# Keeping the residual transposed: a hybrid decoder layer rewritten to feature-major order

## The chip, the cores and the metric

The kernel runs on the 8 cores of one Trainium2 chip. Each core handles one prompt of 2048 tokens and 16 of the 128 sample sequences, with all the weights. The metric is the device time of the slowest core in microseconds (us), as the median over runs. A program on all 8 cores has a second, slower state in some runs, in which cores of one die show a lower granted clock than the others. Those runs are marked slow and are not compared here.

Engine names in the profile: PE is the matrix engine and PEld its weight loads, DVE the vector engine, ACT the scalar (activation) engine, POOL the GpSimd engine, and SP the engine that here only issues transfers. `L376` is line 376 of that kernel. "PEclk" is the clock granted to PE, as a fraction of full speed.

## The reference

One decoder layer: a norm, an input projection (1024 to 2048), two mixers side by side (pooling means, and a gated short convolution), an output projection, a second norm, a squared-ReLU MLP (1024 to 4096 to 1024), and a final norm. Cut to what matters:

```python
def rmsnorm(x, g):
    return x * rsqrt(mean(x * x, axis=-1) + EPS) * g

hn = rmsnorm(x, norm1_g)
u, bg, cg, hc = split(einsum('btd,de->bte', hn, w_in), 4)       # each 512 wide
ya = pool_mixer(u)          # means over the last 2, 4, 8, 16 rows minus u, times pool_w
yb = bg * conv3(cg * hc)    # 3 taps along the tokens
x = x + concat([ya, yb]) @ w_out
hn = rmsnorm(x, norm2_g)
x = x + square(relu(hn @ w1)) @ w2
y = rmsnorm(x, final_g)
```

Per core this is 16 meta + 2048 prompt + 64 sample tokens.

## The kernel before

The residual lies token-major: 128 tokens on the partitions, 1024 features along each row, 17 tiles, of which the last (the 64 sample tokens) is half filled. A norm is then a row sum, which ACT makes together with the square. But the kernel's projections take the features on the partitions, so each normalized tile goes through 8 transposes on PE.

```python
def stats(src, pn, src_keys, junk, junk_key):          # one norm: a row sum on ACT
    P.add("scalar", lambda e: e.activation(out=junk[0:pn, :], in_=src, func=AF.Square,
                                           accum_out=ss[0:pn, slot:slot + 1]), ...)
    ...                                                # Sqrt on ACT, reciprocal on DVE

def transpose_to_fm(hn, hn_key, pn, gT, dst, dst_keys):
    for k in range(8):
        P.add("tensor", lambda e, k=k: e.transpose(out=psT[tb][:, k * 128:k * 128 + pn],
                                                   in_=hn[:, k * 128:(k + 1) * 128], ...), ...)
    ...                                                # DVE: times the gain, out of PSUM

# the pooling sums and their last two steps run on POOL
P.add("gpsimd", lambda e, ...: e.tensor_tensor(out=dstb[:, a0:L], in0=cur_src[:, a0:L],
                                               in1=cur_src[:, a0 - step:L - step], op=ALU.add), ...)

def load_block(b):                                     # MLP weights, block b of 4
    P.dma("gpsimd", ... W1B[i] ...)
    P.dma("gpsimd", ... W2B[i] ...)

load_block(0)
w1_step(0, pending)
pop_pending(pending, 8)
load_block(1)                                          # only after the first step's work is queued
```

All weights come through the casting queue that POOL issues to. The cuts are marked by `...`.

## Time and profile before

| | before |
|---|---|
| time, median of 6 runs | 728.21 us (727.29 to 729.3) |
| profiled span, slowest core | 725.3 us |
| PE busy | 675.0 us, 93% |
| MLP's first matmul | 246.9 us |
| MLP, first to last matmul | 470.5 us |
| after the last matmul | 7.9 us |

The page of the kernel before. The rows of digits are 40 equal slices of the span, each digit the busy share in tenths.

```profile
span 725.3 us, 10524 instructions; the slowest of 8 cores (720.2 to 725.3 us)
...
PE 675.0 (93%) x3705; PEld 320.7 (44%) x3705; DVE 321.8 (44%) x440; ACT 239.3 (33%) x456; POOL 99.4 (14%) x121
...
PE   0699899899899999999999999999999999999995
...
POOL 4184055055073000000000000000000000000000
PEclk9999999999999999999999999999999999999998
...
PE 89%; DMA 4%; ACT 2%; issue 2%; DVE 2%; SPq 0%; ACTq 0%; DVEq 0%
```

PE is the bound: it is busy in 93% of the span, its row is 9 nearly everywhere after the first two slices, and the chain of waits (the last line) goes 89% through it. PEclk is 9 up to the last slice, so little is lost to the clock either. POOL is busy almost only in the first 13 slices, which are the mixer.

Two consecutive pieces of the chain of waits (start, length, what), from the mixer:

```profile
102.00 6.91 PE psall L363 x32
108.91 0.45 PE psall L353 x8
```

Here 32 matmuls of 512 columns take 6.91 us, which is 216 ns each, and 8 transposes of 128 columns take 0.45 us, which is 56 ns each. In stretches without waits, the starts of neighbouring matmuls stand 29 ns apart at 64 columns and 216 at 512 in this kernel's trace (216 for the half-filled tile too). All of these fit columns / 2.4 + 2.5 ns within 0.5 ns, and estimates below are made with that. Each matmul has a weight load of its own, 98 ns long in the mean of its records, and the short ones still start 29 and 56 ns apart.

Busy time by stage (window, its length, then busy us of each engine, granted clock, share of the DMA engines, GB/s):

```profile
0.00:246.90 246.90, 207.77 (x1305) 104.29 (x1305) 115.83 (x173) 129.86 (x240) 93.98 (x115) 0.99 0.37 76
246.90:717.40 470.50, 467.20 (x2400) 216.45 (x2400) 201.96 (x263) 108.11 (x213) 5.39 (x7) 1.00 0.25 48
717.40:725.30 7.90, 0.00 (x0) 0.00 (x0) 3.98 (x5) 1.35 (x3) 0.00 (x0) 0.69 0.49 200
```

In the MLP, PE is idle for only 3.3 of 470.5 us. In the mixer it is idle for 39 of 246.9 us, most of it while the first loads and norms run.

The timeline around a POOL addition (start, length, engine, line, operation):

```profile
111.90 4.25 POOL L474 TENSOR_TENSOR big<-big 128x526 f32<-128x526 f32 x3
...
112.41 1.36 DVE L515 SCALAR_TENSOR_TENSOR big<-big 128x512 f32<-128x512 f32 x1
...
113.70 1.54 DVE L512 SCALAR_TENSOR_TENSOR big<-big 128x512 f32<-128x512 f32 x1
```

POOL adds here from 111.90 to 116.15, three times in a row, 1.42 us each. The two DVE operations beside them, which read two operands from SBUF, take 1.36 and 1.54 us. Elsewhere, with POOL quiet, the same DVE operation took 0.75 us (at 127.2 us), and a POOL addition with DVE quiet took 1.04 us (at 98.2 us). Beside each other, one addition and one DVE operation so get done about every 1.45 us, which is less than the 1.79 us of one after the other.

### The profile page before, as it was taken

The numbers are of one execution on the slowest core, as the hardware profiler recorded it, in microseconds if no ns is written. First come the engines' busy times: TensorE is split into PE (matmuls) and PEld (weight loads), VectorE is DVE, ScalarE is ACT, GpSimd is POOL, SyncE is SP. The second block draws the span as 40 slices with busy tenths as digits, with TensorE's granted clock in tenths as the row PEclk, the third lists the DMA queues.
The fourth block names the chain that finished last, engine by engine and source line by source line (L and its number), as shares of the span: only waits on it lengthen the run. The fifth ranks groups of instructions, "written<-read, shape, count | busy, mean of one in ns | idle before, by whom it ended". The sixth has DMA issues, their size and how long they took to land.

```text
span 725.3 us, 10524 instructions; the slowest of 8 cores (720.2 to 725.3 us)
## 1 busy us (share of the span) xinstructions
PE 675.0 (93%) x3705; PEld 320.7 (44%) x3705; DVE 321.8 (44%) x440; ACT 239.3 (33%) x456; POOL 99.4 (14%) x121
## 2 busy tenths in 40 slices
PE   0699899899899999999999999999999999999995
PEld 0355444444444454444444444444444444444442
DVE  0326527628536453333343333333433333364566
ACT  3655556556443531202012021102220202333432
POOL 4184055055073000000000000000000000000000
PEclk9999999999999999999999999999999999999998
DMA  8994400300002899001643000607000000020224
GB/s 198 190 188 67 148 1 1 117 0 2 1 1 30 122 156 160 30 0 19 98 62 56 0 1 1 107 10 117 1 1 0 2 1 1 1 95 37 88 89 171
DMA packets 19682, 42.98 MB, mean 59 GB/s; under 512 B 1503, under 2 KB 5631, under 8 KB 19616
## 3 DMA queue, kind: packets, MB, share of 16 engines
q0 software_dynamic: 14176, 23.22, 21.2%
q1 hardware_dynamic: 5456, 19.11, 7.7%
q8 instruction: 30, 0.49, 0.3%
q14 instruction: 20, 0.16, 0.1%
HBM read 56.64 MB, written 9.24 MB: 91 GB/s over the span
## 4 chain that ended last, share of the span: by engine, by line
PE 89%; DMA 4%; ACT 2%; issue 2%; DVE 2%; SPq 0%; ACTq 0%; DVEq 0%
PE psall L363 48%; PE psall L743 32%; PE psall L634 6%; DMA big<-w 2%; PE psall L353 2%; DMA big<-xp 2%; DVE big L357 1%; ACT big L346 1%; ACT big L334 1%; ACT big L621 0%; DVE big L762 0%; ACT big L726 0%; ACT big L752 0%; PE psall L595 0%; PE psall L589 0%
## 5 line engine op out<-in xcount | busy, mean ns | idle before, releaser
L363 PE MATMUL psall<-big 128*128 128x512 bf16 (+2 forms) x2036 | 361.5, 335 | 10.9 <-ACT big L726 3.0
L363 PEld LDWEIGHTS psall<-big 128*128 128x128 bf16 x2036 | 167.1, 98 | 194.9 <-issue 18.2
L743 PE MATMUL psall<-big 128*128 128x512 bf16 (+1 forms) x1088 | 238.0, 379 | 0.0
L726 ACT ACTIVATE big<-psall 128x512 f32<-128x512 f32 (+1 forms) x160 | 83.3, 522 | 319.4 <-PE psall L363 310.1
L743 PEld LDWEIGHTS psall<-big 128*128 128x128 bf16 (+1 forms) x1088 | 106.6, 98 | 127.6 <-issue 1.7
L728 DVE TENSOR_TENSOR big<-big 128x512 bf16<-128x512 f32 (+1 forms) x160 | 95.2, 599 | 136.1 <-ACT big L726 135.3
L748 DVE TENSOR_TENSOR big<-psall,big 128x1024 f32<-128x1024 f32 (+1 forms) x68 | 83.3, 1224 | 129.3 <-PE psall L743 127.1
L634 PE MATMUL psall<-big 128*128 128x512 bf16 (+1 forms) x272 | 61.1, 385 | 3.7 <-DVE big L357 3.6
L474 POOL TENSOR_TENSOR big<-big 128x512 f32<-128x512 f32 (+13 forms) x50 | 50.5, 1009 | 79.7 <-ACT big L498 68.5
L357 DVE TENSOR_TENSOR big<-psall,big 128x1024 bf16<-128x1024 bf16 (+2 forms) x35 | 39.8, 1163 | 26.9 <-PE psall L353 26.8
L334 ACT ACTIVATE big<-big 128x1024 bf16<-128x1024 f32 (+2 forms) x35 | 36.9, 1056 | 44.0 <-DVE big L639 35.8
L346 ACT ACTIVATE big<-big 128x1024 bf16<-128x1024 f32 (+2 forms) x35 | 39.4, 1145 | 14.3 <-PE psall L353 9.4
L634 PEld LDWEIGHTS psall<-big 128*128 128x128 bf16 (+1 forms) x272 | 26.9, 100 | 37.3 <-issue 7.4
L353 PE MATMUL psall<-big 128*128 128x128 bf16 (+2 forms) x280 | 21.9, 226 | 15.6 <-ACT big L346 13.9
L752 ACT ACTIVATE big<-big 128x1024 bf16<-128x1024 f32 (+1 forms) x17 | 18.0, 1057 | 42.6 <-DVE big L760 38.4
L639 DVE TENSOR_TENSOR big<-psall,big 128x1024 f32<-128x1024 f32 (+1 forms) x17 | 20.8, 1224 | 22.3 <-PE psall L634 22.3
L353 PEld LDWEIGHTS psall<-big 128*128 128x128 bf16 (+2 forms) x280 | 18.0, 102 | 22.8 <-issue 18.8
L524 DVE TENSOR_TENSOR big<-psall,big 128x512 f32<-128x512 f32 (+2 forms) x24 | 12.5, 526 | 31.3 <-PE psall L363 23.4
L707 POOL DMA_DIRECT2D big<-w x4 | 3.6, 896 | 166.0 <-PE psall L743 160.9
L762 DVE SCALAR_TENSOR_TENSOR big<-big 128x1024 f32<-128x1024 f32 (+1 forms) x17 | 21.8, 1284 | 1.8
L484 POOL TENSOR_TENSOR big<-big 128x512 bf16<-128x512 f32 (+1 forms) x20 | 21.6, 1080 | 3.4 <-PE psall L363 1.3
L339 DVE RECIPROCAL big<-big 128x1 f32<-128x1 f32 (+2 forms) x35 | 5.5, 158 | 34.3 <-ACT big L336 34.3
(48 smaller groups left out, 154.3 us busy)
## 6 DMA issues: line engine op xcount, KB each, us to landing
big<-w POOLq DMA_DIRECT2D x8, 2048.0 KB, 17.5
big<-xp SPq DMA_DIRECT2D x4, 2048.0 KB, 11.7
yp<-big SPq DMA_DIRECT2D x16, 512.0 KB, 2.7
big<-w_in POOLq DMA_DIRECT2D x4, 1024.0 KB, 27.6
big<-w_out POOLq DMA_DIRECT2D x1, 2048.0 KB, 55.8
big<-fg SPq DMA_DIRECT2D x1, 512.0 KB, 3.4
big<-sp SPq DMA_DIRECT2D x2, 240.0 KB, 14.2
nps<-sp SPq DMA_DIRECT2D x1, 352.0 KB, 11.4
```

Source lines behind the costliest of these rows:

```text
L334: P.add("scalar", lambda e: e.activation(out=junk[0:pn, :], in_=src, func=AF.Square, accum_out=ss[0:pn, slot:slot + 1]), reads=src_keys, w ...
L346: P.add("scalar", lambda e: e.activation(out=hn, in_=src, func=AF.Copy, scale=rs[0:pn, slot:slot + 1]), reads=src_keys + [("rs", slot)], w ...
L353: P.add("tensor", lambda e, k=k: e.transpose(out=psT[tb][:, k * 128:k * 128 + pn], in_=hn[:, k * 128:(k + 1) * 128], identity=identb[0:pn, ...
L357: P.add("vector", lambda e: e.tensor_tensor(out=dst, in0=src, in1=gT.unsqueeze(2).to_broadcast([128, 8, pn]), op=ALU.mult), reads=[TK[tb], ...
L363: P.add("tensor", lambda e, k=k: e.matmul(out=psFM[b][:, 0:N], lhsT=lhs_fn(k), rhs=rhs_fn(k), start=(k == 0), stop=(k == nk - 1)), reads=r ...
L474: P.add("gpsimd", lambda e, dstb=dstb, cur_src=cur_src, a0=lo, step=step: e.tensor_tensor(out=dstb[:, a0:L], in0=cur_src[:, a0:L], in1=cur ...
L634: P.add("tensor", lambda e, k=k, kk=kk, half=half, i=i, pn=pn, tb=tb: e.matmul(out=psTM[tb][0:pn, half * 512:(half + 1) * 512], lhsT=MIX[: ...
L726: P.add("scalar", lambda e, ri=ri, ps=ps: e.activation(out=RB[ri][:, 0:N], in_=ps, func=AF.Relu), reads=[("ps", bk)], writes=[("RB", ri)] ...
L728: P.add("vector", lambda e, ri=ri, fc=fc: e.tensor_tensor(out=A2T[ai][:, fc, 0:N], in0=RB[ri][:, 0:N], in1=RB[ri][:, 0:N], op=ALU.mult), r ...
L743: P.add("tensor", lambda e, fc=fc, half=half, i=i, pn=pn, tb=tb: e.matmul(out=psTM[tb][0:pn, half * 512:(half + 1) * 512], lhsT=A2T[ai][:, ...
L748: P.add("vector", lambda e, x1=x1, pn=pn, tb=tb: e.tensor_tensor(out=x1, in0=psTM[tb][0:pn, :], in1=x1, op=ALU.add), reads=TMK[tb] + [("X1 ...
L762: P.add("vector", lambda e: e.scalar_tensor_tensor(out=x1, in0=x1, scalar=rs[0:pn, slot:slot + 1], in1=FG[0:pn, :], op0=ALU.mult, op1=ALU. ...
```

## The change

The intent is to take off PE everything that is not a projection. The residual is kept transposed (8 blocks of 128 features on the partitions, tokens along the columns), so no transposes are needed. All tokens, samples included, are packed in five column groups, so there is no half-filled tile. The pooling weights are folded into the output weights. The host lays the inputs out in the order in which they are read, by permutation only. The input weights come in full precision through SP's hardware queue and are cast on ACT and DVE.

The price: a norm is now a sum across partitions. ACT squares the 8 blocks, POOL adds the 8 squares, PE multiplies the sum with ones, ACT makes the reciprocal root, and DVE scales 8 blocks. A list scheduler with hand-written costs puts the operations of DVE, ACT and POOL in order. The diff rewrites nearly the whole file; its core, with cuts marked:

```diff
+GROUPS = ((16, 496, 0), (0, 432, 64), (0, 480, 0), (0, 480, 0), (0, 160, 0))   # meta, prompt, sample columns
...
+    def tt(out, a, b, op=ALU.add, eng="vector"):
+        cost = 0.1 + out.n / 960 if eng == "vector" else 0.15 + out.n * 1.8e-3
...
-    def stats(src, pn, src_keys, junk, junk_key):
-        slot = nxt("slot", NSLOT)
-        P.add("scalar", lambda e: e.activation(out=junk[0:pn, :], in_=src, func=AF.Square, accum_out=ss[0:pn, slot:slot + 1]),
...
-    def transpose_to_fm(hn, hn_key, pn, gT, dst, dst_keys):
...
+    def sumsq(xs, sq, s, i, n, eng):
+        b = sq[i % sq.shape[0], 0:n]
+        if i == 0:
+            act(s[0:n], xs, AF.Square)
+        else:
+            act(b, xs, AF.Square)
+            tt(s[0:n], s[0:n], b, eng=eng)
+
+    def rstd(s, hl, rs, n, rq=None):
+        act(hl[0, 0:n], s[0:n])
+        tt(hl[1, 0:n], s[0:n], hl[0, 0:n], ALU.subtract)
+        b = bank()
+        mm(b(0, n), ONES[:], hl[0, 0:n], True, False)
+        mm(b(0, n), ONES[:], hl[1, 0:n], False, True)
+        act(rs, b(0, n), AF.Ln, bias=EPS)
...
+    def OUT(g, hook={}):
...
+            tt(x, b(0, n), x)
+            sumsq(x, SQ, Sub(S2, g % 2), d, n, "gpsimd")
...
+    def norm1(g):
+            sumsq(X[g][k], SQ, S1, k, NIN[g], "vector" if g == 0 else "gpsimd")
...
+    def h2_of(g):
+        nm, n = GROUPS[g][0], NOUT[g]
+        rstd(Sub(S2, g % 2), HL, R2N[0:n], n)
+        for k in range(8):
+            stt(H2[g][k, 0:n], X[g][k, nm:nm + n], g2(k), R2N[0:n], ALU.mult, ALU.mult)
...
+    load_w1(0)
+    w1_step(0)
+    load_w2(0)
+    h2_of(NG - 1)
+    load_w1(1)
+    load_w2(1)
```

`tt` is an operation of two tensors, `stt` one of two tensors and a scalar (always on DVE), `mm` a matmul, `act` an operation on ACT.

## The prediction

> **What bounds the kernel now.** TensorE. The page has it busy 675 of 725 us on the slowest core. The chain of waits goes 89% through it, and the core list shows a granted clock of 0.994 to 0.995. Its pieces in the chain: 64 matmuls of 512 columns in 13.81 us (215.8 ns each), 8 transposes of 128 columns in 0.45 us (56 ns), 48 of 64 columns in 1.62 us (34 ns). That is columns/2.4 + 2.5 ns[...]; short matmuls are not held up by weight loads. The rest, in the chain and stage windows: about 38 us of PE work in the first 79 us (so about 40 us lost to loading and normalizing), about 11 us of small mixer waits, 8 us of tail. The MLP begins at about 247 us.
>
> **What the change does to TensorE (estimates from that rate).** The 280 transposes go (-15.7), as do the half-filled sample tile (17 full-width tiles become 2112 columns: W2 235 to 228.5, output projection 59 to 57), the meta and sample matmuls of 32 and 64 columns, and the pool matmuls (-3.5; folded into the output weights, +1.7). Added: the ones-matmuls of the norms, +5.4. In all: input projection 115, output projection 57, W1 228.5, W2 228.5, small 7: 636, against about 665 before. MLP alone: 457 against 465.
>
> **Start.** Input weights now come as f32 through the hardware queue (342 GB/s when busy, from the page's queue table; the casting queue 302 GB/s of source) and are cast by ACT and DVE. The first group needs 2.5 MB, so real matmuls start at 11 to 13 us; then 0.5 MB per 1.6 us keeps just ahead of a weight slot's 1.7 us. Gain: 25 to 28 us, if nothing else bound.
>
> **What takes some back: DVE and POOL in the mixer.** Instruction groups: DVE 0.69 us per 512 from PSUM, ACT 0.59, POOL add 1.04. A two-SBUF-input DVE operation takes 0.75 us alone, but 1.35 to 1.54 us beside a POOL add (timeline at 111 to 117 us; the add goes to 1.48). [...] The new mixer has per full group 28 such DVE operations, 12 to 20 from PSUM and about 24 POOL adds: about 40 to 43 us of DVE against 39 us of PE, and the first two groups, back to back with scaling of every chunk, need about 73 us of DVE against 54 of PE. I put 25 us of PE waits in the mixer: 8 by the end of group 1, 8 before group 2, the rest later. The MLP stays dense (DVE about 11 of 27 us per step).
>
> **Sum.** Start 12 + mixer PE 178 + waits 25 + MLP 457 + waits 2 + tail 7 = 681 us of span, near 683 us of time. Range 664 to 703. Faster by over 2%: 0.94; within 2%: 0.05; slower: 0.01.
>
> **What would show it.** First real matmul near 12 us; 480-column matmuls at 202 ns, 160-column ones at 69 ns; MLP from its first to its last matmul about 457 us, PE over 98% busy; MLP beginning near 215 us; in the mixer PE waiting for DVE, with DVE over 85% busy up to 90 us and its two-input operations over 1 us; tail 6 to 7 us.
>
> **What would make it wrong.** 160-column matmuls held to the 98 ns of a weight load (+20 us over 700 of them). [...] Less clash of DVE and POOL than assumed, or the scheduler's order hiding it (665), or static orders built on too small costs (700).

Two remarks that cite no trace or run of this case are cut from the forecast, and so is a risk of slower loads (+10 us), whose threshold no run shows. No term of its sum is among them: 12 + 178 + 25 + 457 + 2 + 7 = 681 us stands in full. Its 34 ns for 64 columns is the mean of a piece with one gap of 109 ns in it; beside that gap they stand 29 ns apart.

## The result, and the profile after

| | before | changed |
|---|---|---|
| time, median | 728.52 us (20 runs) | 727.01 us (10 runs, one of them slow) |
| ratio of fast runs | | 0.9972, interval 0.9952 to 0.9992 |
| profiled span | 725.3 us | 725.8 us |
| MLP's first matmul | 246.9 us | 240.0 us (predicted 215) |
| MLP, first to last dense matmul | 470.5 us | 472.4 us (predicted 457 + 2) |
| after that | 7.9 us | 13.4 us (predicted 7) |

A ratio is the mean time of one kernel's fast runs over that of the other's in the same rounds, so it is not quite the ratio of the medians. The changed kernel computes the right result.

The page of the changed kernel:

```profile
span 725.8 us, 11301 instructions; the slowest of 8 cores (716.7 to 725.8 us)
...
PE 665.1 (92%) x3648; PEld 340.7 (47%) x3648; DVE 408.0 (56%) x675; ACT 211.3 (29%) x409; POOL 215.9 (30%) x268
...
PE   6977879689969879999999999999999999999981
...
POOL 0496868949578300000000000100000000413460
PEclk8887989989999998999999999999999999999997
...
PE 72%; DVE 8%; POOL 6%; DMA 5%; issue 5%; ACT 2%; POOLq 0%; DVEq 0%; ACTq 0%; SPq 0%
```

PE is still 92% busy, yet the chain of waits goes only 72% through it; POOL, DVE and DMA have come in. POOL's busy time has more than doubled (99 to 216 us), and it now also works at the end of the span. The PEclk row has 7s and 8s inside the span where it had 9s. PE busy time fell by just 10 us instead of the 29 that the removed matmuls are worth, mostly because a matmul at half clock counts as busy for twice as long (at 18 us those of 512 columns stand 427 ns apart, from 22.4 us on 216 ns). Another 7 us are 24 warm-up matmuls before the first data, which the changed kernel has and the prediction's sum did not name.

The same three stages:

```profile
0.00:240.00 240.00, 202.13 (x1011) 96.89 (x1012) 175.30 (x268) 96.31 (x178) 166.49 (x215) 0.91 0.37 98
240.00:712.40 472.40, 462.38 (x2638) 243.60 (x2635) 223.68 (x381) 112.68 (x225) 49.45 (x54) 0.99 0.21 44
712.40:725.80 13.40, 0.62 (x3) 0.21 (x2) 9.06 (x27) 2.31 (x7) 0.00 (x0) 0.60 0.52 179
```

Set against the prediction's sum (215 + 459 + 7 = 681), the span of 725.8 us is 25 us longer in the mixer, 13.4 us longer in the MLP, and 6.4 us longer in the tail. Each of the three has its own cause, so they are taken one at a time.

**The mixer.** What PE waited for over the whole run (who, total us, times, longest):

```profile
PE psall L376 <- ACT big L386: 25.7, 8, 5.9
PE psall L376 <- DVE big L391: 12.5, 9, 6.1
PE psall L376 <- DVE big L409: 9.2, 8, 2.4
PE psall L376 <- DMA big<-w: 5.1, 1, 5.1
```

The mixer's matmuls by shape, from the first one with data at 9.5 us to 240 us, are 106 of 512 columns, 295 of 496, 392 of 480 and 194 of 160. At columns / 2.4 + 2.5 ns that is 177.4 us (an estimate from the rate that both traces show), and the prediction said 178. The stretch takes 230.5 us, so 53 us are lost in it, where the prediction left 25. Of these 53 us, PE is idle 35, and 18 are matmuls that took longer than that rate, most of them at half clock (195.2 us busy against 177.4).

Where the lower clock lies is seen in windows of 5 us after a wait (the last three columns are granted clock, DMA share, GB/s; the count behind PE's busy time is its matmuls):

```profile
140.00:145.00 5.00, 0.00 (x0) 0.00 (x0) 5.00 (x7) 1.64 (x4) 5.00 (x5) 0.68 0.00 0
145.00:150.00 5.00, 2.65 (x7) 0.94 (x8) 4.11 (x7) 2.11 (x5) 3.69 (x7) 0.50 0.00 0
150.00:155.00 5.00, 5.00 (x21) 2.14 (x20) 4.89 (x9) 1.36 (x3) 0.19 (x1) 0.80 0.00 0
155.00:160.00 5.00, 5.00 (x26) 2.33 (x25) 5.00 (x7) 1.24 (x2) 2.76 (x2) 1.00 0.00 0
```

PE waits from 139.5 to 145.4 us. In the next two windows it runs 7 matmuls (with one more wait of 1.9 us among them) and 21, at a granted clock of 0.50 and 0.80, and only then is the rate of 26 back. On this core the clock drops to 0.50 in or right after each of the six waits of 3.6 us or more (3.6 to 6.1 us, at 60 to 717 us), and in two clusters of shorter waits, at 10 to 16 us and at 48 to 53 us; two waits of 2.5 and 2.0 us, which end at 702 and 710 us, bring no drop. The recorded stretches at 0.50 last 3.4, 6.8 or 10.2 us, and the last one, at the end of the span, 12.7 us. Summed up they cover 64 us, 13 of them at the very end, against 11 in the kernel before, 7 of them at the end. PE was not always idle ahead of a drop: it was busy for 1.0, 1.4 and 1.2 us of the 3.4 us ahead of the drops at 12.1, 49.6 and 141.8 us.

What stood before that wait (timeline; behind the count is the idle time and who ended it):

```profile
136.97 4.42 DVE L400 SCALAR_TENSOR_TENSOR big<-big 128x496 bf16<-128x496 f32 x3
...
137.86 4.59 POOL L391 TENSOR_TENSOR big<-big 128x480 f32<-128x480 f32 x3
...
143.00 1.61 POOL L391 TENSOR_TENSOR big<-big 128x480 f32<-128x480 f32 x1
...
144.70 0.60 ACT L386 ACTIVATE big<-big 128x480 bf16<-128x480 f32 x1 [1.49 <-POOL big L391]
...
145.45 0.56 PE L376 MATMUL psall<-big 128*128 128x480 bf16 x1 [5.92 <-ACT big L386]
```

POOL makes three additions of a norm's squares at 1.53 us each, while DVE's two-input operations take 1.47 us each. After a last addition of 1.61 us, ACT makes the bf16 copy of the sum, and only then may PE go on; it has waited 5.92 us. The costliest groups of the mixer show the same as means (busy us, mean ns, idle before, releasers):

```profile
L391 POOL TENSOR_TENSOR big<-big 128x480 f32<-128x480 f32 x36 | 47.5, 1323 | 13.4 <-ACT big L386 11.3 <-POOL big L391 1.8
...
L400 DVE SCALAR_TENSOR_TENSOR big<-big 128x496 f32<-128x496 f32 x8 | 12.5, 1588 | 0.0
```

The POOL group holds norm additions, for the larger part, and pooling sums. A POOL addition of 480 columns takes 1.32 us on average, not the 1.04 us for 512 that it takes alone, and eight DVE operations took 1.59 us instead of 0.75.

**The MLP.** The chain of waits around the one long wait in it:

```profile
241.64 31.12 DMA big<-w
...
273.00 3.05 PE psall L376 x7
```

The MLP is otherwise dense, but PE stands still for 5.1 us before 273.0 us: the second weights of block 0 were issued at 241.6 us and landed 31.1 us later. From 205 to 245 us eleven transfers went to that queue; the nine ahead of its two halves were the first weights of blocks 0 and 1 and half of the second weights of block 1.

**The tail.** A stretch of the chain of waits in the last block:

```profile
698.20 1.07 POOL big L391
...
699.46 0.87 POOL big L391
```

POOL's additions of the final norm's squares, one after the other at 0.70 to 1.07 us, are on the chain from 694 to 708 us.

### The profile page after: what moved, and what is told of

Same layout as the page of the kernel before. It is cut to its first block, busy times and chain, and to the rows that moved or that the text cites. A ratio compares the mean times of both kernels' runs of the same rounds, so it can differ in the third digit from the quotient of the medians.

```text
span 725.8 us, 11301 instructions; the slowest of 8 cores (716.7 to 725.8 us)
## 1 busy us (share of the span) xinstructions
PE 665.1 (92%) x3648; PEld 340.7 (47%) x3648; DVE 408.0 (56%) x675; ACT 211.3 (29%) x409; POOL 215.9 (30%) x268
## 3 DMA queue, kind: packets, MB, share of 16 engines
q1 hardware_dynamic: 12192, 27.17, 11.1%
## 4 chain that ended last, share of the span: by engine, by line
PE 72%; DVE 8%; POOL 6%; DMA 5%; issue 5%; ACT 2%; POOLq 0%; DVEq 0%; ACTq 0%; SPq 0%
PE psall L376 72%; POOL big L391 6%; DVE big L400 5%; DMA big<-w 4%; DVE big L391 3%; ACT big L386 2%; DMA big<-x 1%; DVE big L409 1%; POOL big L415 0%; DVEq L248 0%; ACT L386 0%; ACT big L414 0%; POOLq L248 0%; POOLq L229 0%; ACTq L248 0%
## 5 line engine op out<-in xcount | busy, mean ns | idle before, releaser
L376 PE MATMUL psall<-big 128*128 128x480 bf16 (+4 forms) x3648 | 665.1, 345 | 55.0 <-ACT big L386 25.7
L376 PEld LDWEIGHTS psall<-big 128*128 128x128 bf16 x3648 | 340.7, 99 | 379.2 <-issue 87.0
L391 POOL TENSOR_TENSOR big<-big 128x480 f32<-128x480 f32 (+15 forms) x166 | 178.3, 1084 | 244.3 <-ACT big L386 203.5
L391 DVE TENSOR_TENSOR big<-psall,big 128x480 f32<-128x480 f32 (+9 forms) x272 | 152.5, 572 | 138.1 <-PE psall L376 125.2
L386 ACT ACTIVATE big<-psall 128x480 f32<-128x480 f32 (+4 forms) x208 | 105.7, 517 | 328.3 <-PE psall L376 286.1
L391 DVE TENSOR_TENSOR big<-big 128x480 bf16<-128x480 f32 (+5 forms) x190 | 113.2, 599 | 144.4 <-ACT big L386 142.9
L400 DVE SCALAR_TENSOR_TENSOR big<-big 128x480 bf16<-128x480 f32 (+10 forms) x184 | 140.9, 804 | 23.2 <-ACT big L386 11.7
L386 ACT ACTIVATE big<-big 128x480 f32<-128x480 f32 (+10 forms) x190 | 98.0, 536 | 169.8 <-DVE big L391 100.7
L415 POOL COPY big<-big 128x16 f32<-128x16 f32 (+1 forms) x72 | 27.2, 392 | 6.7 <-DVE big L400 4.2
L414 ACT CAST big<-big 128x1024 bf16<-128x1024 f32 x10 | 10.2, 1038 | 2.9 <-DMA big<-w_in 2.9
```

Source lines behind the costliest of these rows:

```text
L376: return P.add("tensor", lambda e: e.matmul(out=out.ap, lhsT=w.ap, rhs=x.ap, start=start, stop=stop), reads=[w, x], writes=[out], cost=max ...
L386: return P.add("scalar", lambda e: e.activation(out=out.ap, in_=in_.ap, func=func, scale=sc, **kw), reads=reads, writes=[out], cost=0.14 + ...
L391: return P.add(eng, lambda e: e.tensor_tensor(out=out.ap, in0=a.ap, in1=b.ap, op=op), reads=[a, b], writes=[out], cost=cost)
L400: return P.add("vector", lambda e: e.scalar_tensor_tensor(out=out.ap, in0=a.ap, scalar=sv, in1=b.ap, op0=op0, op1=op1), reads=reads, write ...
L414: return P.add(eng, lambda e: e.copy(out=out.ap, in_=a.ap), reads=[a], writes=[out], cost=0.14 + n / 1200)
L415: return P.add(eng, lambda e: e.tensor_copy(out=out.ap, in_=a.ap), reads=[a], writes=[out], cost=0.15 + n / 960)
```

## The experiments

Eleven kernels were run, each on all 8 cores. The rival theories at the start:

- **A:** the half clock after the waits is what costs. Keep PE busy in the waits, and the slow stretches come back as time.
- **B:** at half clock PE only gives DVE and POOL time to catch up. At full clock it would stand sooner at the next wait.
- **C:** the mixer waits for the latency of the norms: square, 7 additions, matmul, logarithm, exponential, one after the other.
- **D:** the mixer is bound by the amount of work on DVE and POOL. Take away one wait, and it returns at another.
- **E** (added for e6 and e8): DVE alone has too much to do, and POOL's part doesn't matter.
- **F** (added after the first four runs): the scheduler's costs are too small, and it is their bad order that makes the waits.

The kernel before, which ran beside e1 to e8 and e11, had fast runs from 728 to 739 us on those chips. This makes the intervals of the ratios wide and the verdicts of e1 to e8 "unclear" (only e9 and e11 are "faster", and e10 has none), though the kernels' own fast runs agree within 0.4%. So the ratio is given, and the gain is read from the median of the fast runs against the changed kernel's 727.0. The fastest run of the kernel before was 726.8 us on the chips of the main comparison, and 728.7, 728.1, 728.2 and 728.6 us on the four others, so these chips agree within 0.3%. The changed kernel itself was not run again on the four others, so a gain against its 727.0 is uncertain by about 2 us; e5 to e8 ran on one chip and can be compared with each other more closely. e1 to e4 ran on one chip, e5 to e8 on a second, e9 and e10 on a third, e11 on a fourth.

### e1_fill: useless matmuls in five long waits

```diff
+    def idle_mm(b, m):
+        for _ in range(m):
+            mm(b(0, 512), ONES[:], FILL[0:512], True, True)
...
         b = bank()
+        idle_mm(b, m)          # 16, 28, 14 ahead of the sums of groups 1, 3, 4
         mm(b(0, n), ONES[:], hl[0, 0:n], True, False)
...
+            if si == 0 and d == 0:
+                idle_mm(bk, 20)          # ahead of the first W2 step
...
+                if g == 0 and i == 0 and k in (2, 4, 6):
+                    idle_mm(wb, 5)       # while the first weights arrive
```

> The changed kernel, with matmuls of no use (ones times a constant) put into five of TensorE's waits: 15 between the first group's row blocks, 16, 28 and 14 ahead of the norm matmuls of groups 1, 3 and 4, and 20 ahead of the first W2 step. Outputs stay right. Theory A (after each wait of 3 us or more TensorE runs at a granted clock of 0.50 for some 6 to 8 us): these stretches shrink, the mean granted clock of the slowest core rises from 0.957 to 0.975 or more, and the time falls by 8 to 16 us, to 711 to 719, although TensorE has 93 matmuls more to do. Theory B (the lost time is the waits themselves, and the low clock falls in stretches where TensorE would wait anyway): the time stays within 4 us of 727 or rises. One wait that can't be filled, about 6 us for PSUM banks ahead of the folding of the pool weights, stays and keeps its slow stretch in both.

(Theory A's 3 us and 6 to 8 us are round figures. The trace of the changed kernel has the drops at waits of 3.6 to 6.1 us, and stretches of 3.4 to 10.2 us before the tail.)

Correct; 722.5 us in the three fast runs, ratio 0.9846 [0.9756, 0.9937]. The granted clock of the cores, 0.957 to 0.965 in the changed kernel, rose to 0.974 to 0.979. The MLP began at 236.3 us instead of 240.0 on the slowest core, and at 236.7 instead of 238.2 as the mean of the 8 cores. The gain of 4.5 us lies between the two theories, nearer to B: of the 18 us by which the matmuls of the mixer took longer, 2 to 4 came back there. The half clock is mostly a follower of the waits, not a cost of its own.

### e2_load_order: the second weights of block 0 first

```diff
-    load_w2(0)
+    first = load_w2(0)
     h2_of(NG - 1)
-    load_w1(1)
-    load_w2(1)
+    load_w1(1, first)          # issued after both halves of W2(0) have landed
+    load_w2(1, first)
```

> The changed kernel, with the W1 load of block 1 and the W2 load of block 1 issued only when the W2 load of block 0 has landed. Theory (the queue is first come first served and full at about 150 GB/s written, 300 GB/s of source, from 217 to 273 us, so that the W2 load of block 0 stands behind loads that are not needed for 70 us): the 5.2 us wait of TensorE for a weight load at 268 us goes away, and with it the half-clock stretch after it (about 3 us): 7 to 9 us faster, 718 to 720. Rival (the load is late because its place in the buffer is freed late, at the end of the output projection): the wait shrinks by less than 2 us and the time stays within 2 us of 727.

(In the changed kernel's trace the twelve weight loads issued to that queue from 216.9 to 264.4 us land in the order of their issue, from 223.6 to 277.6 us. The DMA engines moved 139 GB/s on average from 217 to 273 us, at a busy share of 0.9 or more from 220 us on.)

Correct; 719.6 us, ratio 0.9811 [0.9761, 0.9861]. The window that held the wait, 240 to 272 us (columns as before):

```profile
240.00:272.00 32.00, 32.00 (x159) 15.17 (x157) 20.95 (x37) 11.30 (x23) 6.77 (x13) 1.00 0.79 115
```

PE is busy in all 32.00 us, where the changed kernel had 27.85 us, and no wait for a transfer is left in the list of waits. The gain of 7.4 us fits the wait of 5.1 plus the half clock behind it. As expected.

### e3_tail: the last norms summed on PE

```diff
+        if g >= NG - 2:
+            b = bank()
+            for k in range(8):
+                mm(b(0, n), ONES[:], SQP[sf][k, 0:n], k == 0, k == 7)
...
-            if b == NBLK - 1:
+            if b == NBLK - 1 and g >= NG - 2:
+                act(SQP[fin[0] % 2][d, 0:n], x, AF.Square)     # bf16
```

> The changed kernel, with the last norm of groups 3 and 4 summed by TensorE (squares written in bf16, eight ones-matmuls) and not by adds on POOL and DVE. Theory (from 693 us on the chain goes through 14 POOL adds of 0.7 to 0.9 us, and TensorE waits 4.9 us in two places for their sums; then the last two norms and their scalings queue on DVE): those POOL adds go, the waits at 702 and 710 us go, and the end from the last W2 matmul to the last instruction falls from 13.4 us to 9 to 11: 6 to 9 us faster in all, 718 to 721. Rival (the tail is bound by DVE's scalings, 8 of each half group, whatever makes the sums): 3 us or less.

Correct; 720.1 us, ratio 0.9816 [0.9765, 0.9867]. Eight matmuls with ones take the place of the seven additions and the split. The waits for POOL's sums at the end are gone, and the gain is 6.9 us. As expected.

### e4_no_norm_wait: PE no longer waits for the sums (wrong result)

```diff
-        mm(b(0, n), ONES[:], hl[0, 0:n], True, False)
-        mm(b(0, n), ONES[:], hl[1, 0:n], False, True)
+        mm(b(0, n), ONES[:], FILL[0:n], True, False)
+        mm(b(0, n), ONES[:], FILL[0:n], False, True)
```

> Wrong result on purpose: the ones-matmuls of all norms read a constant in place of the sums, so nothing waits for a norm's sum; all squares, adds and casts are still done. Theory C (a good half of TensorE's waits are places in its fixed program order where a norm's matmul waits for a long ACT, POOL, ACT, DVE chain, though DVE and POOL as a whole would keep up): the waits at 64, 145, 213, 237, 702, 710 and 717 us go with the half-clock stretches after them: 20 to 35 us faster, 692 to 707. Theory D (the mixer is bound by the work of DVE and POOL, as predicted; the norm is only where the backlog shows): the same backlog comes up as waits for PSUM banks, and the mixer ends no more than 8 us earlier; gain 8 to 18 us, most of it in the tail.

The result is wrong, as meant: a constant stands for the sums, which are still computed. 719.8 us, ratio 0.9804 [0.9742, 0.9867]; the MLP began at 233.3 us, only 6.7 us sooner. What PE waited for:

```profile
PE psall L377 <- DVE big L392: 15.1, 12, 4.1
...
PE psall L377 <- DMA big<-w: 6.9, 2, 3.9
PE psall L377 <- ACT big L387: 4.6, 6, 1.1
```

The waits for ACT, which are those for the norms, fell from 25.7 to 4.6 us. But the waits for DVE to free a PSUM bank (L392, which was L391) rose from 12.5 to 15.1 us, now twelve of them. With 6.7 of the 25 us gained, C explains the smaller part, and D stands (it had said at most 8 us there, and 8 to 18 us in all, of which 7.2 falls just short). The scheduler, freed of these dependencies, also put DVE, ACT and POOL in another order, so the 6.7 us are not the waits' alone. The waits for the last norms went too, while the wait for the second weights grew to 6.9 us, so the gain of 7.2 us in time is not the mixer's alone.

### e5_both: e2 and e3 together

The edit is the sum of the two diffs above. It is the base of e6 to e8.

> The load order of e2 and the tail of e3 together, right outputs. If the two losses are separate, as the traces show them (one at 268 to 277 us, one after 693 us), the gains add: 727.0 - 7.4 - 6.9 = 712.7, within 2 us. If one hid the other: 716 or more. The mixer should end near 240 us as before. The next three runs are built on this kernel.

Correct; 713.0 us, ratio 0.974 [0.9674, 0.9806]. The two gains add up (14.0 against 7.4 + 6.9), and the MLP still begins at 239.0 us. So the MLP's load and the tail are independent of the mixer's loss.

### e6_pe_sums: all norms of the mixer summed on PE

```diff
-            sumsq(x, SQ, Sub(S2, g % 2), d, n, "gpsimd")
+            act((SQI if g == NG - 1 else SQO)[d, 0:n], x, AF.Square)
...
-            sumsq(X[g][k], SQ, S1, k, NIN[g], "vector" if g == 0 else "gpsimd")
+            act(SQI[k, 0:NIN[g]], X[g][k], AF.Square)
...
+    def rstd_pe(sq, rs, n, rq=None):
+        b = bank()
+        for k in range(8):
+            mm(b(0, n), ONES[:], sq[k, 0:n], k == 0, k == 7)
```

> e5 with the norms of the mixer (both norms, all groups) summed by TensorE: squares in bf16, eight ones-matmuls each; about 70 POOL adds of 1.2 us and the split in high and low parts go, TensorE gets about 10.6 us more of matmuls. Right outputs. Theory D (the mixer is bound by the work of DVE and POOL, which slow each other): POOL's busy time before 240 us falls from about 170 to 90 us, the mean of DVE's two-input operations (about 1.0 to 1.2 us of 480 to 496 elements) falls below 0.95, and the mixer ends 12 to 25 us earlier in spite of the added matmuls: 690 to 701. Theory E (DVE alone has too much to do; POOL's part doesn't matter): the mixer ends less than 5 us earlier or later: 708 to 720.

Correct; 695.0 us, ratio 0.9498 [0.9433, 0.9562]. Its first two stages:

```profile
0.00:222.10 222.10, 206.13 (x1063) 100.53 (x1064) 145.67 (x252) 90.42 (x169) 92.15 (x150) 0.95 0.41 103
222.10:680.00 457.90, 457.90 (x2623) 242.15 (x2621) 217.14 (x368) 110.08 (x217) 36.99 (x41) 1.00 0.25 46
```

The MLP begins at 222.1 us although PE was given some 10.6 us more matmuls (an estimate from their columns). POOL is busy 92 us in the mixer, against 164.8 us in e5. DVE's 120 scalar-and-two-tensor operations in the mixer fell from 867 to 718 ns on average. The clock came with it: 0.95 in the mixer instead of 0.91, without a single filler matmul. PE waits 16 us in all. D holds. But the edit also took some 12 us of additions and splits of the norms off DVE itself, so it doesn't rule out E; e8 and e11, which leave DVE all its instructions, do.

### e7_costs: the same work, ordered with measured costs

```diff
-        cost = 0.1 + out.n / 960 if eng == "vector" else 0.15 + out.n * 1.8e-3
+        cost = 0.15 + out.n / 960 if eng == "vector" else 0.25 + out.n * 2.1e-3
...
-                     reads=reads, writes=[out], cost=0.1 + out.n / 960)        # stt
+                     reads=reads, writes=[out], cost=0.25 + out.n * 1.4e-3)
```

> e5, scheduled with costs nearer to the measured ones (POOL add 0.25 us + 2.1 ns per element, two-input DVE operation 0.25 + 1.4 ns, small POOL copy 0.36 us), which changes only the order of instructions on DVE, ACT and POOL. Theory F (the order, built on costs that are 40% too small, makes engines wait for each other): the mixer ends 10 us or more earlier: 703 or less. Theory D (the work itself): within 5 us of e5 either way.

Correct; 705.0 us, ratio 0.9631 [0.955, 0.9711], MLP from 232.4 us. The gain of 8 us over e5 lies between what the theories said (at least 10, at most 5). The order, made from costs that were too small, is a second and smaller cause.

### e8_short_pool: POOL's norm additions cut to 32 columns (wrong result)

```diff
-            tt(s[0:n], s[0:n], b, eng=eng)
+            m = 32 if eng == "gpsimd" else n
+            tt(s[0:m], s[0:m], sq[i % sq.shape[0], 0:m], eng=eng)
```

> e5 with wrong results on purpose: POOL's adds of the norms in the mixer cover 32 columns and not the whole group, so all waits and their order stay and only their length goes (about 1.2 us to 0.25 each). Theory D: the two-input operations of DVE get shorter (mean below 0.95 us) and the mixer ends 15 to 30 us earlier: 683 to 698. Theory E (DVE alone): less than 6 us. Against e6 it tells what the added matmuls cost.

The result is wrong, as meant. All instructions are kept; only the POOL additions are short. 681.8 us, ratio 0.932 [0.9257, 0.9383]. Its first two stages, and the shortened group:

```profile
0.00:212.10 212.10, 194.01 (x1011) 94.96 (x1012) 159.40 (x268) 96.48 (x178) 112.49 (x210) 0.96 0.41 108
212.10:670.00 457.90, 457.90 (x2621) 242.18 (x2619) 214.55 (x372) 110.72 (x218) 18.75 (x44) 1.00 0.24 47
```

```profile
L392 POOL TENSOR_TENSOR big<-big 128x32 f32<-128x32 f32 x60 | 21.2, 353 | 48.1 <-ACT big L387 46.4 <-POOL big L392 1.6
```

DVE's scalar-and-two-tensor operations in the mixer of e5, of e6 and of e8:

```profile
L401 DVE SCALAR_TENSOR_TENSOR big<-big 128x480 bf16<-128x480 f32 (+9 forms) x120 | 99.7, 867 | 19.6 <-POOL big L392 10.9 <-ACT big L387 8.2
...
L399 DVE SCALAR_TENSOR_TENSOR big<-big 128x480 bf16<-128x480 f32 (+9 forms) x120 | 80.8, 718 | 17.4 <-POOL big L390 11.8 <-ACT big L385 4.9
...
L401 DVE SCALAR_TENSOR_TENSOR big<-big 128x480 bf16<-128x480 f32 (+9 forms) x120 | 84.8, 753 | 8.6 <-ACT big L387 4.4 <-POOL big L392 3.4 <-POOL big L416 0.4
```

The MLP begins at 212.1 us; the prediction said 215. That is 27 us sooner than in e5, where E allowed 6, so DVE's work alone is not it. The 60 additions of the mixer take 353 ns each, which with all else takes 52 us off POOL (112.5 us busy against 164.8 in e5), so they took about 1.2 us each before. The DVE group falls from 99.7 us in e5 to 84.8. This run also shows the MLP bare: 457.90 us of PE busy in 457.90 us. e6 does the same work correctly and is 13 us slower, of which the added matmuls are an estimated 10.6.

The run has a flaw: the scheduler reckoned with the shorter additions, so the order on DVE, ACT and POOL changed too, and theory F could claim a part of the gain. Hence e11.

### e11_short_order: e8 in the order of e5 (wrong result)

```diff
+    def tt(out, a, b, op=ALU.add, eng="vector", nc_=None):
...
-            tt(s[0:n], s[0:n], b, eng=eng)
+            m = 32 if eng == "gpsimd" else n
+            tt(s[0:m], s[0:m], sq[i % sq.shape[0], 0:m], eng=eng, nc_=n)   # scheduled with the cost of n columns
```

The order of the instructions on every engine was compared with that of e5 beforehand and is the same. The kept traces agree: on core 1 the kinds of instruction follow each other as in e5 on PE, DVE, ACT and POOL, while in e8 66 of DVE's 665 places hold another kind.

> e8 with one thing undone: the POOL norm additions cover 32 columns (wrong result on purpose), but the list scheduler is still told their full cost, so every engine keeps exactly the order of e5; in e8 the order had changed with the costs. Theory D (the length of POOL's additions, with their slowing of DVE, is the loss): MLP from 212 to 217 us and a time of 682 to 688 us, nearly all of e8's gain. Theory F (the order is what costs, and e8 gained by a new one): MLP from 222 us or later, a time of 692 us or more.

681.0 us (680.9 to 681.4), ratio 0.9275 [0.9197, 0.9352]. The windows around the MLP's first matmul, which is the 1011th:

```profile
0.00:205.00 205.00, 188.70 (x962) 90.91 (x963) 153.99 (x261) 92.32 (x169) 111.90 (x205) 0.96 0.42 110
205.00:208.00 3.00, 2.10 (x27) 1.66 (x25) 1.96 (x5) 1.82 (x5) 0.75 (x2) 1.00 0.74 111
208.00:211.00 3.00, 3.00 (x31) 2.34 (x32) 1.75 (x5) 2.29 (x6) 1.25 (x4) 1.00 0.49 49
```

989 matmuls lie before 208.0 us and 1020 before 211.0, so the MLP begins near 210 us, even sooner than expected. The order is that of e5, so the gain of 32 us over e5 is that of the additions' length alone, with what it does to DVE. Counted from 9.5 us as before, what is left in the mixer above 177.4 us of full-rate matmuls is about 23 us, where the prediction put 25. D holds, and F's 8 us of e7 are largely a part of what long additions cost: with short additions the order of e5 (681.0 us) does no worse than the new order of e8 (681.8).

### e9_sums_costs: e6 ordered with the costs of e7

The edit is the sum of those of e2, e3, e6 and e7.

> e6 (norm sums on TensorE, load order, tail) scheduled with the costs of e7. Right outputs. If order and POOL's work are two causes, the gain of e7 over e5 (8 us) comes on top in part: 686 to 692. If the order only mattered because POOL was overloaded: within 2 us of e6's 695.

Correct; 691.1 us (689.3 to 691.9, 5 runs), ratio 0.9468 [0.9444, 0.9492]: faster than both kernels, by 5.3% against the kernel before. Against e6, which ran on another chip, the better order gained 3.9 us, about half of what it gave in e7, as the first expectation said. The page:

```profile
PE 665.5 (96%) x3726; PEld 345.4 (50%) x3726; DVE 373.4 (54%) x648; ACT 204.7 (30%) x396; POOL 127.4 (18%) x191
...
PEclk9898999999999999999999999999999999999997
...
PE 88%; DMA 7%; DVE 2%; SPq 2%; issue 1%; ACT 1%; POOL 1%; DVEq 0%; ACTq 0%; POOLq 0%
```

PE does as many us of work as in the changed kernel, but nearly all of it at full clock (3726 matmuls against 3648), and the chain of waits goes 88% through it again.

### e10_start_fill: e9 with 15 useless matmuls while the first weights arrive

The edit is the last part of that of e1.

> e9 with 15 useless matmuls between the row blocks of the first group only, where TensorE waits for data from 9 to 17 us and then runs at a clock of 0.50 to about 22 us. Theory A (at the start the low clock costs time of its own, since TensorE then has data): the half-clock stretch there goes and the time falls by 2 to 4 us. Theory B (DVE's backlog from the same stage takes it back at the next wait for banks, near 90 us): less than 1 us either way.

Correct; only two of seven runs were fast, at 690.3 and 691.3 us, so there is no ratio. The granted clock between 10 and 22 us is 1.00, where e9 has 0.72, and yet no time is gained against e9's 691.1. This is theory B once more. As means of the 8 cores, the wait near 57 us for a bank that DVE has to free takes 4.8 us instead of 3.8, and the MLP begins at 216.4 us against 216.1 in e9. Two fast runs alone are weak, but in the five slow ones the cores of die 0 were undisturbed, at 687.8 us on average, against 687.1 us for the same cores in e9's runs.

## Why the prediction was wrong, point by point

Predicted and measured, as positions of the profiled span:

| | predicted | changed | e5 | e6 | e8 | e11 | e9 |
|---|---|---|---|---|---|---|---|
| MLP's first matmul, us | 215 | 240.0 | 239.0 | 222.1 | 212.1 | 210 | 219.4 |
| from there to the end, us | 466 | 485.8 | 470.7 | 470.8 | 469.0 | 469 | 470.9 |
| time, us | 683 | 727.0 | 713.0 | 695.0 | 681.8 | 681.0 | 691.1 |

The positions are those of the slowest core. As the mean of the 8 cores, the MLP's first matmul is at 238.2 us in the changed kernel, 237.6 in e5, 220.7 in e6, 209.5 in e8, 208.3 in e11 and 216.1 in e9, so the differences are nearly the same.

**Right: what bounds the kernel before, and the rates.** The matmul rate held at every width (69 ns from start to start at 160 columns, 202.5 at 480, 209 at 496). In e8 the 2621 matmuls after 212.1 us, a fifth of them of 160 columns, took 457.9 us without a gap; the prediction said 457. A 160-column matmul held to the 98 ns of a weight load (the mean on the page before) would have made it about 15 us more (512 matmuls times 29 ns), which did not come. The mixer's matmuls were worth 177.4 us against 178 said. The first one with data came at 9.5 us against 11 to 13. The loads at the start moved 327 GB/s in the windows from 9.5 to 17.5 us, against the forecast's 342 when busy.

**Wrong: "I put 25 us of PE waits in the mixer".** This is the step that failed; it measured 53. The prediction named the right pair of engines, DVE and POOL slowing each other, but it had the path wrong. It set DVE's load against PE's and let PE wait where DVE ran out of time. Its own mark for that, "DVE over 85% busy up to 90 us", did not come true: DVE was busy 74% of those 90 us, and itself sat waiting for ACT and POOL. What it left out is that 60 POOL additions stand in series with the squares, the matmul and the scaling of the norms, so PE waits for POOL through ACT and DVE: of the 35 us that PE stood idle, 17 ended with ACT's copy of a norm's sum. And it listed a POOL addition at 1.04 us (1.48 beside DVE) but put no time down for POOL; the mixer shows 1.3 us on average and up to 1.7 for each.

e6 and e11 show that the additions are the cause: with them off POOL the mixer is 17 us shorter than in e5, even with more matmuls, and with them shortened, in the same order, it is 29 us shorter. e4 shows that it is not the wait for the sums alone (6.7 us).

**Wrong: nothing was put down for the clock.** PE's clock stood at 0.50 in or right after each wait of 3.6 us or more. Most of 18 of the 53 us in the mixer were spent so. e1 and e10 show that this is not 18 us to be had back by keeping the clock up: most of it was time in which DVE and POOL caught up. When the waits went (e6), the clock rose by itself.

**Foreseen as a risk: "static orders built on too small costs".** The changed kernel's costs give a POOL addition of 480 columns 1.01 us and DVE's 0.6 us, against 1.32 and 0.87 measured as means. e7 gained 8 us by the costs alone.

**Wrong: "waits 2" in the MLP.** The second weights of block 0 landed behind weights that were not needed until block 1. The prediction read the queue's rate and not its order. It cost 7.4 us (e2).

**Wrong: "tail 7".** It measured 13.4 us, with more waits before it. The last norms sum 8 squares on POOL, whose additions are serial, where the kernel before had a row sum on ACT. It cost 6.9 us (e3).

**The sum.** 25 + 13.4 + 6.4 = 45 us above the predicted span. The mixer is 25 of them. From the MLP's first matmul on, the changed kernel takes 485.8 us where 466 were predicted, and e5 takes 470.7, so e2 and e3 together account for 15 of those 20 us. e8 and e11 still take 469 us there; these last 3 us were not looked into. In e8 they lie after the MLP's last dense matmul, where 11.1 us pass and not 7.

**Open.** How much of the mixer's loss is the slowing of DVE by POOL, and how much is POOL's own length in series, was not separated: e8 and e11 shorten both at once. The DVE group's fall from 99.7 to 84.8 us in e8 puts the slowing at some 15 us of DVE time, which need not all be PE time. No run kept POOL's length while taking away DVE's second operand.

## What to carry to other kernels

Work taken off the saturated engine gained here only as much as the engines that took over its duties could keep up (727.0 us as built, 681.0 with POOL's additions cut short in e11): cost their operations in the company they will have, not alone, and count a chain of small operations as latency too. A sum across 8 blocks of 128 partitions costs PE 8 matmuls with ones (about 1.6 us at 480 columns, an estimate from the 202.5 ns of one) in place of 7 POOL additions of 1.3 us each. Where PE had free slots while POOL stood in the chain, that was the cheaper place, as e6 and e9 show (695.0 and 691.1 us, against 713.0 in e5). Check a new load order for what lands behind what. And if a clock drops after waits, remove the wait and not the drop: filling waits with matmuls gained 4.5 us (e1), the norm sums on PE, with which its waits came to 16 us in all, gained 18 (e6 against e5).
